# A gated group norm whose factors go to the partitions through memory instead of through products with the identity

## The chip, the core and the metric

The kernel runs on one core of a Trainium2 chip. A core has TensorE (PE, matrix products into PSUM), VectorE (DVE), ScalarE (ACT), GpSimd (POOL) and SyncE (SP, which here issues nearly all DMAs), each with its own queue of instructions, worked off in order. The metric is the device time of one execution in microseconds (us), lower is better.

## What is computed

Two layers of a decoder trunk over 512 tokens of 1024 channels, float32: a Mamba-2 mixer and a feed-forward block, then a recurrent mixer and a feed-forward block, each between RMS norms. The change lies in the first mixer, after its scan:

```python
def gated_group_rmsnorm(y, z, w):
    bsz, s, d = y.shape                                   # d = 2048
    g = (y * jax.nn.silu(z.astype(jnp.float32))).reshape(bsz, s, SSD_GROUPS, d // SSD_GROUPS)
    g = g * lax.rsqrt(jnp.mean(g * g, axis=-1, keepdims=True) + EPS)
    return g.reshape(bsz, s, d) * w.astype(jnp.float32)

def ssd_mixer(u, w_in, conv_w, conv_b, dt_bias, a_log, d_skip, norm_w, w_out):
    proj = u @ w_in
    z = proj[..., :SSD_D_INNER]
    ...
    y = ssd_chunked_scan(xs, dt, a, bm, cm)
    y = y + d_skip.astype(jnp.float32)[:, None] * xs
    y = gated_group_rmsnorm(y.reshape(bsz, s, SSD_D_INNER), z, norm_w)
    return (y.astype(u.dtype) @ w_out).astype(u.dtype)
```

So each of 4 groups of 512 channels has one factor for each of the 512 tokens.

## The kernel before

Activations lie with channels over the 128 partitions and the 512 tokens along the free dimension; y of the mixer is 16 such tiles, 4 to a group, held in pairs in the buffers named w and v. Every large product is made of three fp32r products of split operands (high times high, high times low, low times high): `up_mm` (L241 to L248) makes 24 matmuls for a tile of 128 output channels, and `Weight` (L214 to L236) loads 512 KB of weights through SP (L220) into one of 4 buffers r, and splits it with ACT (L227) and DVE (L228).

`ssd` (L333) walks over the 4 groups. For each group `scan_group` works through 4 chunks of 128 tokens. `scores` loads cs_d spread over the partitions (L435), makes products L437, turns y tiles with the identity (L443), and computes decays on ACT (L459, L460, L466) and DVE (L439, L445, L461, L467). `products` makes the short products L477 and L479 and adds their result to y on DVE (L486). Between the chunks stand "fill" units: projections with convolution for the next group (`conv_tile`: ACT L327, DVE L329, ACT L415, DVE L416), and the gate of the group before.

`gate(g)` has three steps. `project` multiplies y by silu(z) and sums the squares of the 4 tiles into one tile, sq, of 128 partitions by 512 tokens (DVE L525, L528; ACT L524, L529; POOL L533). `rate` sums sq over the partitions with a column of ones (L540, result r: tokens on partitions, 4 columns), adds eps on DVE (L541) and raises it to -1/2 on POOL (L543). Then r must get from "token on the partition" to "token along the free dimension, the same on all partitions": `rate` copies r along the free dimension into sq (L544), and `scale` multiplies that by the identity on PE (L550), so that the factors stand in a PSUM bank, which DVE reads while it scales the 4 tiles of y (L554). The four gates are called "places" below: the first runs in the fill of group 2, the second in that of group 3, the third after the last scan, and the fourth among the products with the output weights (L665), after which ACT and DVE split the scaled y (L259, L260).

The order on each engine is made by a scheduler at build time, which places instructions by its own estimate of when they can run. PSUM banks are split into 4 for projections (M) and 4 for the rest (X), each handed out in turn; the narrow buffers t come in a pool of 5 for projections and gates (C2).

Of the kernel before, what the change touches and what calls it, by code (L numbers as in the profile page):

```python
# [8 lines left out]
F32 = mybir.dt.float32  # L9
F32R = mybir.dt.float32r  # L10
AF = mybir.ActivationFunctionType
ALU = mybir.AluOpType

P = 128
D = 1024
S = 512
KD = D // P
NT = S // P
DI = 2048
NH = 32  # L20
NG = 4
# [54 lines left out]
def tile_trunk(ctx: ExitStack, tc: tile.TileContext, x, norm_mix_pre, norm_mix_post, norm_ffn_pre, norm_ffn_post,  # L76
               ssd_w_in, ssd_conv_w, ssd_conv_b, ssd_dt_bias, ssd_a_log, ssd_d, ssd_norm, ssd_w_out,
               lru_w_in, lru_b_in, lru_conv_w, lru_conv_b, lru_w_gx, lru_b_gx, lru_w_ga, lru_b_ga,
               lru_lambda, lru_w_out, lru_b_out, ffn_w_up, ffn_conv_w, ffn_conv_b, ffn_w_down, out, layers=4):
# [3 lines left out]
    V, A, G, T = nc.vector, nc.scalar, nc.gpsimd, nc.tensor  # L83
    dma = nc.sync.dma_start
# [44 lines left out]
    ident, nhalf, ones = (small_tiles[n] for n in ("ident", "nhalf", "ones"))  # L129
# [8 lines left out]
    def small():  # L138
        return stats[:, stat_ids.pop(0), :]
# [98 lines left out]
    def up_w(w, c0, n=P, lo=None, hi=None):  # L238
        return Weight([w[:, c0:c0 + n].rearrange("(k p) c -> p k c", p=P)], KD, KD * n, lo, hi)

    def up_mm(pt, w, h, tok, m=P, by_k=True):  # L241
        o = pt.ap[0:m, :].rearrange("p (a b) -> p a b", a=2)[:, tok, :]
        hh, hl = (a[:, tok, :, :] for a in h)
        ops = ((w.wh, hh), (w.wh, hl), (w.wl, hh))
        todo = [(k, i) for k in range(KD) for i in range(3)] if by_k else [(k, i) for i in range(3) for k in range(KD)]
        for n, (k, i) in enumerate(todo):
            last = T.matmul(o, ops[i][0][:, k, :], ops[i][1][:, :, k, :], start=(n == 0), stop=(n == 3 * KD - 1))  # L247
        return last  # L248
# [84 lines left out]
    def ssd(h, prep, fetch, epilogue):  # L333
        w_in, w_out = ssd_w_in[0], ssd_w_out[0]
        M, X = PS.take(4), PS.take(4)
# [3 lines left out]
        def y_of(m):  # L339
            return y[m // 2].ap[:, cols(m % 2)]  # L340
# [6 lines left out]
        pt = M.get()  # L347
# [30 lines left out]
        v, e_, z, z2, p_, one = (s.ap[0:NH, :] for s in ts_)  # L378
# [11 lines left out]
        pt = X.get()  # L390
# [7 lines left out]
        pt = X.get()  # L398
# [113 lines left out]
                cur = nxt  # L512


        def gate(g):
            st = {}

            def project(m):
                w = up_w(w_in, m * P)
                pt = M.get()  # L520
                up_mm(pt, w, h, FULL)
                w.free()
                th = C2.get()
                A.activation(th.ap, pt.ap, AF.Tanh, scale=0.5)  # L524
                V.scalar_tensor_tensor(out=th.ap, in0=th.ap, scalar=1.0, in1=pt.ap, op0=ALU.add, op1=ALU.mult)  # L525
                pt.free()
                ym = y_of(m)
                V.scalar_tensor_tensor(out=ym, in0=th.ap, scalar=0.5, in1=ym, op0=ALU.mult, op1=ALU.mult)  # L528
                A.activation(th.ap, ym, AF.Square)  # L529
                if m == 4 * g:  # L530
                    st["sq"] = th
                else:
                    G.tensor_tensor(out=st["sq"].ap, in0=st["sq"].ap, in1=th.ap, op=ALU.add)  # L533
                    th.free()

            def rate():
                sq, r = st["sq"], small()
                pt = X.get()
                for t in range(NT):
                    T.matmul(pt.ap[:, t:t + 1], sq.ap[:, t * P:(t + 1) * P], ones[:, 0:1], start=True, stop=True)  # L540
                V.tensor_scalar(out=r, in0=pt.ap[:, 0:NT], scalar1=1.0 / 512, scalar2=EPS, op0=ALU.mult, op1=ALU.add)  # L541
                pt.free()
                G.tensor_tensor(out=r, in0=r, in1=nhalf, op=ALU.pow)  # L543
                V.tensor_copy(sq.ap.rearrange("p (a b) -> p a b", a=NT), r.unsqueeze(2).to_broadcast([P, NT, P]))  # L544

            def scale():
                sq = st["sq"]
                pt = X.get()
                for t in range(NT):
                    T.matmul(pt.ap[:, t * P:(t + 1) * P], sq.ap[:, t * P:(t + 1) * P], ident, start=True, stop=True)  # L550
                sq.free()
                for m in range(4 * g, 4 * g + 4):
                    ym = y_of(m)
                    V.scalar_tensor_tensor(out=ym, in0=ym, scalar=consts["clru"][:, 100 + m:101 + m], in1=pt.ap, op0=ALU.mult, op1=ALU.mult)  # L554
                pt.free()

            return [lambda m=m: project(m) for m in range(4 * g, 4 * g + 4)], rate, scale

        def conv_units(g):
# [24 lines left out]
        with behind(marks + turned), tc.issue_after(first_fetch.ins):  # L584
            dma(dall, ssd_d.to_broadcast([P, NH]))
            for e in range(2):
                V.tensor_copy(dch[64 * e:64 * e + 64, :], dall[64 * e:64 * e + 64, :].rearrange("p (m e) -> p e m", e=2)[:, e, :])
            rows_late()
        gates = [gate(g) for g in range(NG)]
        for g in range(NG):  # L590
            nxt = conv_units(g + 1) if g < NG - 1 else None
# [3 lines left out]
            elif g < NG - 1:  # L595
                z, rate, scale = gates[g - 1]
                z, u = list(z), fill
# [10 lines left out]
        z, last_rate, last_scale = gates[NG - 1]  # L608
        z[0]()
        gates[NG - 2][1]()  # L610
        z[1]()
        gates[NG - 2][2]()
        z[2]()
        z[3]()


        ya = []
# [199 lines left out]
    consts = {}  # L817
# [115 lines left out]
    for ph in range(layers):  # L933
# [26 lines left out]
        if ph == 0:  # L960
            ssd(h, prep, fetch, epilogue)
        elif ph == 2:
            lru(h, prep, fetch, epilogue)
        else:
            ffn(ph // 2, h, prep, fetch, epilogue)
# [31 lines left out]
```

## Time and profile before

| | us |
|---|---|
| median of 3 runs | 1641.8 (1641.77 to 1642.23) |
| the profiled execution | 1640.5 |
| its span in the profile | 1638.7 |
| PE busy | 1626.4 |
| DVE busy | 925.3 |
| ACT busy | 705.0 |
| POOL busy | 175.2 |

Busy time is per engine; the engines overlap. PE's weight loads (PEld) run beside its products. The granted clock of PE is at full in all 40 slices of the page. A row of a timeline merges instructions of one line that follow each other, and its brackets say how long the engine stood idle before the row and what ended that. The first mixer takes about the first 400 us of the span.

### The profile page before, as it was taken

To read this page: it belongs to the slowest core of one execution; us is meant where nothing else is said; L and a number is where in the kernel's file an instruction comes from. 1 tells how busy PE (TensorE), PEld (TensorE's weight loads), DVE (VectorE), ACT (ScalarE), POOL (GpSimd) and SP (SyncE) were. 2 spreads that over 40 slices of the span, in tenths; PEclk is the share of its full clock that TensorE was granted. 3 is DMA by queue.
4 is the path that set the end of the run, shared out by engine and by line. 5 is a ranking of instruction groups with operands and counts; after the bars stand their busy time and mean duration, and the time that the engine had idled before them with its cause. 6 is when DMAs were issued, how large, how long until landed. Compare 5 with 4: busy or idle time off the path is not lost.

```text
span 1638.7 us, 20013 instructions
## 1 busy us (share of the span) xinstructions
PE 1626.4 (99%) x7925; PEld 1352.9 (83%) x7925; DVE 925.3 (56%) x1204; ACT 705.0 (43%) x1036; POOL 175.2 (11%) x194
## 2 busy tenths in 40 slices
PE   8999999999999999999999999999999999999998
PEld 7877887888888888888888988879888888888886
DVE  7979888546644444443343687967444444443342
ACT  5476754334533333332333478546333333333331
POOL 1023113102111111100000100011111101100001
PEclk9999999999999999999999999999999999999999
DMA  7444441333623322323334033436322323233321
GB/s 206 113 122 115 117 120 47 103 104 99 179 81 94 87 83 85 90 91 103 104 116 129 14 107 101 129 94 167 91 84 83 90 79 101 78 90 96 119 69 52
DMA packets 235419, 165.21 MB, mean 101 GB/s; under 512 B 6576, under 2 KB 219292, under 8 KB 235327
## 3 DMA queue, kind: packets, MB, share of 16 engines
q1 hardware_dynamic: 235038, 163.68, 34.5%
q8 instruction: 62, 1.02, 0.3%
q14 instruction: 31, 0.25, 0.0%
q10 hardware_dynamic: 288, 0.26, 0.0%
HBM read 161.76 MB, written 2.16 MB: 100 GB/s over the span
## 4 chain that ended last, share of the span: by engine, by line
PE 95%; DMA 2%; ACT 1%; DVE 1%; POOL 1%; issue 0%; SPq 0%; POOLq 0%; DVEq 0%; ACTq 0%
PE ps L247 60%; PE ps L270 25%; PE ps L665 5%; DMA w<-cs_d 1%; PE ps L188 1%; PE ps L477 1%; PE ps L479 1%; PE ps L491 0%; ACT w L459 0%; POOL t L533 0%; PE ps L443 0%; PE ps L699 0%; PE ps L700 0%; PE ps L701 0%; PE ps L354 0%
## 5 line engine op out<-in xcount | busy, mean ns | idle before, releaser
L247 PE MATMUL ps<-hh,w 128*128 128x512 f32 (+1 forms) x3248 | 945.8, 376 | 0.0
L247 PEld LDWEIGHTS ps<-hh,w 128*128 128x128 f32 x3248 | 592.1, 189 | 110.1 <-issue 3.0
L228 DVE TENSOR_TENSOR w<-r,w 128x1024 fp32r<-128x1024 f32 x281 | 346.6, 1239 | 539.3 <-ACT w L227 329.2
L247 PE MATMUL ps<-hl,w 128*128 128x512 f32 (+1 forms) x1624 | 603.6, 376 | 0.0
L227 ACT ACTIVATE w<-r 128x1024 fp32r<-128x1024 f32 (+1 forms) x280 | 292.9, 1054 | 368.2 <-PE ps L247 149.1
L270 PE MATMUL ps<-w,w 128*128 128x512 f32 x1776 | 405.8, 390 | 0.0
L270 PEld LDWEIGHTS ps<-w,w 128*128 128x128 f32 x1776 | 332.8, 188 | 70.2 <-issue 1.4
L247 PEld LDWEIGHTS ps<-hl,w 128*128 128x128 f32 x1624 | 303.0, 188 | 54.9 <-issue 2.0
L804 POOL TENSOR_TENSOR w<-t,t 128x512 f32<-128x512 f32 x48 | 61.6, 1283 | 461.8 <-DVE t L329 452.2
L329 DVE SCALAR_TENSOR_TENSOR t<-ps,cffn1a,t 128x511 f32<-128x511 f32 (+1 forms) x128 | 95.5, 746 | 17.6 <-ACT t L327 15.5
L329 DVE SCALAR_TENSOR_TENSOR t<-ps,cffn0a,t 128x511 f32<-128x511 f32 (+1 forms) x128 | 95.5, 746 | 15.9 <-ACT t L327 13.8
L327 ACT ACTIVATE t<-ps,cffn1b 128x512 f32<-128x512 f32 x64 | 49.4, 771 | 92.5 <-PE ps L247 92.5
L665 PE MATMUL ps<-w,w 128*128 128x512 f32 x384 | 88.5, 391 | 0.0
L327 ACT ACTIVATE t<-ps,cffn0b 128x512 f32<-128x512 f32 x64 | 49.4, 771 | 90.2 <-PE ps L247 90.2
L665 PEld LDWEIGHTS ps<-w,w 128*128 128x128 f32 x384 | 71.7, 188 | 15.0 <-DVE w L228 0.2
L799 ACT ACTIVATE t<-t 128x512 f32<-128x512 f32 x64 | 40.4, 632 | 92.8 <-DVE t L329 92.8
L259 ACT ACTIVATE w<-w 128x512 fp32r<-128x512 f32 (+1 forms) x62 | 40.2, 650 | 69.2 <-PE ps L270 40.0
L202 POOL TENSOR_SCALAR stats<-stats 128x1 f32<-128x1 f32 x32 | 9.1, 286 | 552.5 <-ACT t L200 552.5
L459 ACT ACTIVATE w<-w,t 128x128 f32<-128x128 f32 x128 | 39.3, 391 | 36.6 <-DMA w<-cs_d 33.6
L329 DVE SCALAR_TENSOR_TENSOR t<-ps,cssd,t 128x511 f32<-128x511 f32 (+2 forms) x72 | 52.4, 737 | 2.5 <-ACT t L327 2.3
L260 DVE TENSOR_TENSOR w<-w,w 128x512 fp32r<-128x512 f32 (+1 forms) x62 | 44.5, 718 | 8.2 <-ACT w L259 8.2
L200 ACT ACTIVATE t<-ps 128x512 f32<-128x512 f32 x32 | 19.1, 598 | 57.9 <-PE ps L270 50.7
(185 smaller groups left out, 904.1 us busy)
## 6 DMA issues: line engine op xcount, KB each, us to landing
r<-in_ffn_w_up_dram SPq DMA_DIRECT2D x128, 512.0 KB, 4.1
r<-in_ffn_w_down_dram SPq DMA_DIRECT2D x64, 512.0 KB, 3.4
r<-in_ssd_w_in_dram SPq DMA_DIRECT2D x40, 512.0 KB, 3.8
r<-in_lru_w_in_dram SPq DMA_DIRECT2D x20, 512.0 KB, 4.9
w<-cs_d SPq DMA_DIRECT2D x16, 512.0 KB, 8.7
r<-in_ssd_w_out_dram SPq DMA_DIRECT2D x16, 512.0 KB, 3.8
r<-in_lru_w_out_dram SPq DMA_DIRECT2D x10, 512.0 KB
out_dram<-xr SPq DMA_DIRECT2D x6, 256.0 KB, 2.0
```

Of the source, the lines that this page charges most:

```text
L227: A.activation(self.hi.ap[:, 0:n], r, AF.Copy)
L228: (lo or V).tensor_tensor(out=self.lo.ap[:, 0:n], in0=r, in1=self.hi.f[:, 0:n], op=ALU.subtract)
L247: last = T.matmul(o, ops[i][0][:, k, :], ops[i][1][:, :, k, :], start=(n == 0), stop=(n == 3 * KD - 1))
L259: A.activation(self.ah, ap, AF.Copy)
L260: V.tensor_tensor(out=self.al, in0=ap, in1=self.ah.bitcast(F32), op=ALU.subtract)
L270: T.matmul(acc[h].ap, x_[:, tk], w_[:, cols(h)], start=(first and i == 0), stop=(last and i == 2))
L327: A.activation(dst, src, AF.Identity, bias=col(k) if bias is None else bias, scale=col(k - 1))
L329: V.scalar_tensor_tensor(out=dst[:, s:S], in0=src[:, 0:S - s], scalar=col(k - 1 - s), in1=dst[:, s:S], op0=ALU.mult, op1=ALU.add)
L459: A.activation(scv[:, e, :], csv[:, e, :], AF.Relu, scale=-1.0, bias=csT[:, c, 8 * g + e:8 * g + e + 1])
L665: T.matmul(acc.ap, a[:, tk], b[:, u, :], start=(j == 0 and u == 0 and i == 0), stop=(j == 7 and u == 1 and i == 2))
L799: A.activation(ga.ap, ga.ap, AF.Gelu_apprx_tanh)
L804: G.tensor_tensor(out=p[-1].ap[:, cols(m % 2)], in0=ga.ap, in1=va.ap, op=ALU.mult)
```

## The change

`rate` no longer copies r into sq. It writes r, 128 partitions by 4 columns, as a row of 512 tokens into a buffer in memory (r_d, one row for each group), and reads that row back into sq, spread over all 128 partitions. Both transfers are issued by SP, and the second waits for the first to have landed. `scale` multiplies y by sq directly, without PE and without a PSUM bank; sq stays in use until the scaling is done. At the end of the scan the scaling of group 2 is written after the last three projections of group 3.

```diff
+        r_d = tc.dram_tile([NG, S], F32, name="r_d")
+
...
                 G.tensor_tensor(out=r, in0=r, in1=nhalf, op=ALU.pow)
-                V.tensor_copy(sq.ap.rearrange("p (a b) -> p a b", a=NT), r.unsqueeze(2).to_broadcast([P, NT, P]))
+
+                dma(r_d[g].rearrange("(t p) -> p t", p=P), r)
+                dma(sq.ap, r_d[g:g + 1].to_broadcast([P, S]))
 
             def scale():
                 sq = st["sq"]
-                pt = X.get()
-                for t in range(NT):
-                    T.matmul(pt.ap[:, t * P:(t + 1) * P], sq.ap[:, t * P:(t + 1) * P], ident, start=True, stop=True)
-                sq.free()
                 for m in range(4 * g, 4 * g + 4):
                     ym = y_of(m)
-                    V.scalar_tensor_tensor(out=ym, in0=ym, scalar=consts["clru"][:, 100 + m:101 + m], in1=pt.ap, op0=ALU.mult, op1=ALU.mult)
-                pt.free()
+                    V.scalar_tensor_tensor(out=ym, in0=ym, scalar=consts["clru"][:, 100 + m:101 + m], in1=sq.ap, op0=ALU.mult, op1=ALU.mult)
+                sq.free()
...
         z, last_rate, last_scale = gates[NG - 1]
         z[0]()
         gates[NG - 2][1]()
-        z[1]()
+        for m in range(1, 4):
+            z[m]()
         gates[NG - 2][2]()
-        z[2]()
-        z[3]()
```

The scheduler makes a new order from this. Three pieces of it follow; each row is a line, an operation, and output and input tiles with their numbers. In the order of the change the lines are those of the changed file (L547 and L548 there are the two transfers; the other lines named here are the same as before).

DVE at the first place, before:

```order
L541 TENSOR_SCALAR stats<-ps_241_1626 128x4
L416 SCALAR_TENSOR_TENSOR v_39_438<-t_247_1666,t_246_1665 128x512
L544 COPY t_170_1197<-stats 128x512
L228 TENSOR_TENSOR w_298_1971<-r_296_1968,w_297_1970 128x1024
L439 TENSOR_TENSOR t_43_445<-ps_258_1745,mask 128x128
L461 TENSOR_TENSOR w_263_1760<-w_263_1760,t_43_445 128x1024
L329 SCALAR_TENSOR_TENSOR t_252_1704<-ps_251_1679,cssd,t_252_1704 128x511
L554 SCALAR_TENSOR_TENSOR w_34_433<-w_34_433,clru,ps_254_1712 128x512 x2
L554 SCALAR_TENSOR_TENSOR w_35_434<-w_35_434,clru,ps_254_1712 128x512 x2
```

and with the change:

```order
L416 SCALAR_TENSOR_TENSOR v_39_438<-t_247_1668,t_246_1667 128x512
L228 TENSOR_TENSOR w_297_1968<-r_295_1965,w_296_1967 128x1024
L554 SCALAR_TENSOR_TENSOR w_34_433<-w_34_433,clru,t_170_1198 128x512
L329 SCALAR_TENSOR_TENSOR t_252_1706<-ps_251_1681,cssd,t_252_1706 128x511
L554 SCALAR_TENSOR_TENSOR w_34_433<-w_34_433,clru,t_170_1198 128x512
L554 SCALAR_TENSOR_TENSOR w_35_434<-w_35_434,clru,t_170_1198 128x512 x2
L486 SCALAR_TENSOR_TENSOR w_36_435<-w_36_435,dch,ps_254_1718 128x128 x2
L486 SCALAR_TENSOR_TENSOR w_37_436<-w_37_436,dch,ps_254_1718 128x128 x2
L439 TENSOR_TENSOR t_43_445<-ps_257_1742,mask 128x128
L329 SCALAR_TENSOR_TENSOR t_252_1706<-ps_251_1681,cssd,t_252_1706 128x510
L467 TENSOR_TENSOR w_281_1871<-w_281_1871,w_158_1138 128x1024
L461 TENSOR_TENSOR w_262_1757<-w_262_1757,t_43_445 128x1024
```

The copy L544 is gone, the first scaling L554 stands where it was the turn of L439 and L461, and these two come after all four scalings and L486.

SP at the first place, before:

```order
L220 DMA r_333_2192<-in_ssd_w_in_dram 128x8x128
L435 DMA w_275_1846<-cs_d 128x8x128
L220 DMA r_340_2239<-in_ssd_w_in_dram 128x8x128
L435 DMA w_302_2007<-cs_d 128x8x128
L435 DMA w_324_2140<-cs_d 128x8x128
```

and with the change:

```order
L220 DMA r_332_2189<-in_ssd_w_in_dram 128x8x128
L435 DMA w_274_1843<-cs_d 128x8x128
L547 DMA r_d<-stats 128x4x1
L548 DMA t_170_1198<-r_d 128x512
L220 DMA r_339_2237<-in_ssd_w_in_dram 128x8x128
L435 DMA w_301_2004<-cs_d 128x8x128
```

The write and the read back stand between a load of cs_d and the next weight load.

PE at the first place, before:

```order
L437 MATMUL ps_258_1745<-w_158_1137 128x128
L247 MATMUL ps_267_1777<-hh_83,w_265_1773 128x512
L247 MATMUL ps_267_1777<-hl_84,w_265_1773 128x512
L247 MATMUL ps_267_1777<-hh_83,w_266_1774 128x512
L247 MATMUL ps_267_1777<-hh_83,w_265_1773 128x512
L247 MATMUL ps_267_1777<-hl_84,w_265_1773 128x512
L477 MATMUL ps_255_1721<-w_230_1547,t_229_1545 64x128
```

and with the change, at the same stretch:

```order
L247 MATMUL ps_251_1681<-hh_83,w_249_1677 128x512
L247 MATMUL ps_251_1681<-hl_84,w_249_1677 128x512
L247 MATMUL ps_251_1681<-hh_83,w_250_1678 128x512
L477 MATMUL ps_254_1718<-w_230_1548,t_229_1546 64x128
L479 MATMUL ps_254_1718<-w_231_1559,t_234_1585 64x128
```

A later stretch of PE with the change, where the y tile v_39 is turned:

```order
L247 MATMUL ps_288_1897<-hh_83,w_286_1893 128x512
L247 MATMUL ps_288_1897<-hl_84,w_286_1893 128x512
L443 MATMUL ps_258_1745<-ident,v_39_438 128x128
L443 MATMUL ps_276_1848<-ident,v_39_438 128x128
L247 MATMUL ps_288_1897<-hh_83,w_287_1894 128x512
```

Before, L437 and five products L247 stood ahead of the short products L477 and L479, and L550 among these; now the short products come first, and L443, which needs the finished tile v_39, comes 71 products L247 after them.

## Rows read from the trace of the kernel before

**Rows 1.** The page: busy time of each engine (share, instructions), and the chain by engine.

```profile
PE 1626.4 (99%) x7925; PEld 1352.9 (83%) x7925; DVE 925.3 (56%) x1204; ACT 705.0 (43%) x1036; POOL 175.2 (11%) x194
...
PE 95%; DMA 2%; ACT 1%; DVE 1%; POOL 1%; issue 0%; SPq 0%; POOLq 0%; DVEq 0%; ACTq 0%
```

**Rows 2.** The chain in order of time: start us, us, engine, tile and line.

```profile
171.76 0.44 DVE t L544
172.24 1.16 PE ps L550 x8
...
194.81 1.03 PE ps L477 x16
...
240.30 0.89 PE ps L550 x8
...
291.41 0.89 PE ps L550 x8
292.30 10.89 PE ps L247 x48
...
336.79 0.89 PE ps L550 x8
```

**Rows 3.** Timeline of PE's weight loads: start us, us; in brackets idle before, and releaser.

```profile
172.24 0.41 PEld L550 LDWEIGHTS ps<-ident,t 128*128 128x128 f32 x3 [0.36 <-DVE t L544]
```

**Rows 4.** Timeline of DVE around the first place, same columns.

```profile
173.23 0.28 DVE L439 TENSOR_TENSOR t<-ps,mask 128x128 f32<-128x128 f32 x1
173.55 1.23 DVE L461 TENSOR_TENSOR w<-w,t 128x1024 f32<-128x1024 f32 x1
176.46 0.75 DVE L329 SCALAR_TENSOR_TENSOR t<-ps,cssd,t 128x511 f32<-128x511 f32 x1 [1.68 <-ACT t L327]
177.13 2.72 DVE L554 SCALAR_TENSOR_TENSOR w<-w,clru,ps 128x512 f32<-128x512 f32 x4
...
180.42 1.12 DVE L486 SCALAR_TENSOR_TENSOR w<-w,dch,ps 128x128 f32<-128x128 f32 x4
181.45 1.22 DVE L467 TENSOR_TENSOR w<-w,w 128x1024 f32<-128x1024 f32 x1
```

**Rows 5.** Timeline of POOL, first place.

```profile
170.32 1.41 POOL L543 TENSOR_TENSOR stats<-stats,nhalf 128x4 f32<-128x4 f32 x1 [10.33 <-DVE stats L541]
```

**Rows 6.** Timeline of SP: first the write of cs_d, then the first place.

```profile
74.43 0.34 SPq L389 DMA_DIRECT2D cs_d<-t  x1
76.07 2.84 SPq L435 DMA_DIRECT2D w<-cs_d  x3
...
173.40 0.37 SPq L220 DMA_DIRECT2D r<-in_ssd_w_in_dram  x1
174.89 4.78 SPq L435 DMA_DIRECT2D w<-cs_d  x2
```

**Rows 7.** DMA view: queue; issues (count, KB each, median us to landing).

```profile
q1 hardware_dynamic: 235038, 163.68, 34.5%
...
w<-cs_d SPq DMA_DIRECT2D x16, 512.0 KB, 8.7
...
out_dram<-xr SPq DMA_DIRECT2D x6, 256.0 KB, 2.0
...
v<-in_norm_mix_post_dram SPq DMA_DIRECT2D x2, 512.0 KB, 3.7
```

**Rows 8.** Timeline of ACT, first place.

```profile
181.01 2.46 ACT L459 ACTIVATE w<-w,t 128x128 f32<-128x128 f32 x8 [1.74 <-DMA w<-cs_d]
...
186.69 0.62 ACT L415 ACTIVATE t<-t 128x512 f32<-128x512 f32 x1
```

**Rows 9.** Timeline of PE, start of the short products of the first place.

```profile
171.25 0.45 PE L477 MATMUL ps<-w,t 128*64 128x128 f32 x4
```

**Rows 10.** Timeline of DVE at the second and the fourth place.

```profile
241.91 2.71 DVE L554 SCALAR_TENSOR_TENSOR w<-w,clru,ps 128x512 f32<-128x512 f32 x4
...
326.00 1.23 DVE L228 TENSOR_TENSOR w<-r,w 128x1024 fp32r<-128x1024 f32 x1 [3.54 <-PE ps L665]
```

## The prediction

> **What bounds the kernel now.** I read the page's busy shares first: TensorE (PE) is busy 99% of 1638.7 us, and 95% of the chain that ended last is PE time, DMA 2% [rows 1]. So an instruction taken off PE shortens the kernel by its own time, and work on other engines counts only where PE comes to wait for it. Then the four places where the group norm runs, one for each group of channels. In the chain in order of time, the products with the identity (L550) stand there with their whole length, and at the first of them the chain passes through the copy that feeds them (L544) [rows 2]. The weight loads of PE show 0.36 us of waiting for that copy [rows 3]. The third view is VectorE's (DVE) own timeline around the first place, since DVE is where the new wait will stand.
>
> **The change, part by part.** *PE.* Sixteen fp32 products go (32 records, 8 to a place): 1.16 + 0.89 + 0.89 + 0.89 = 3.83 us [rows 2], and the wait of 0.36 us before the first goes with them [rows 3]. Two of the four places lie among the short products L477 and L479, where the joins come out slightly differently; I round 4.19 down to 4.0 us. PE's other instructions stay, in another order, and I put that at nothing: the changes from one kind of product to another are nearly as many as before.
>
> *DVE.* Four copies of 0.44 us go [rows 2]. DVE is not the bound, so this is worth nothing by itself. The scaling L554 keeps its instructions, 2.72 us for four [rows 4], and reads SBUF where it read PSUM; I put that at nothing.
>
> *The chain that takes the place of copy and products.* GpSimd (POOL) ends the power at 170.32 + 1.41 = 171.73 at the first place [rows 5]. From there it was 0.44 us of copy and 1.16 us of products. Now SyncE (SP) writes r to memory, waits until it has landed, and issues the read back. The nearest row for the first transfer is the write of cs_d: issued at 74.43, and the first read of it could be issued at 76.07, so 1.64 us [rows 6]. That is the lower end; cs_d goes in 32 rows of 2 KB, r in 512 pieces of 4 bytes. The hardware queue's 235038 packets took 34.5% of 16 engines' 1638.7 us, 38 ns each on average [rows 7]; 512 of them over 16 engines are 32 x 38 ns = 1.2 us, so the upper end is 2.9 us. I take 2.2. The read back is 128 rows of 2 KB, 256 KB. Its nearest rows are out_dram, 256 KB in 2.0 us, and the spread gain norm_mix_post, 512 KB in 3.7 us [rows 7]; I take 2.8. The far row is the spread of cs_d, 512 KB in 8.7 us [rows 7]. With 0.1 us for signals the chain is 5.1 us, between 3.7 and 6.7, and 11.7 at the far end.
>
> The Trainium skill ("DMA: Bandwidth & Descriptors", Rules for kernel authors) says that a strided last dimension lowers to one descriptor per element and should be rearranged, which speaks against this write; the order shows the 128x4x1 pattern, and no row here has a transfer of 4-byte pieces. Its fit (Anatomy of one DMA) of 2.0 us plus bytes at 436 GB/s would give, as an estimate, 2.0 + 2.6 = 4.6 us for the chain, and the same sum below; the write of cs_d at 1.64 us is under its constant.
>
> *SP's queue.* SP issues in order, so whatever stands behind the write waits for POOL, and what stands behind the read waits for the landing. At the first place that is the weight load which went out at 173.40, now about 174.4, and the load of cs_d at 174.89, which keeps its time [rows 6]. At the second and third place the next weight load waits longer for a free buffer anyway; at the fourth one load comes some 3 us later, with weights needed 20 us on. So nothing comes from the queue itself, but at the first place a spread of 256 KB now lies ahead of cs_d in the engines, and I let that data come 1 us later than 181.01, where ScalarE (ACT) waited for it [rows 8].
>
> *The first place.* This is the tight one. By the order DVE now runs L228 and then stands at the first L554 until the chain ends: 171.73 + 5.1 = 176.8. Before, it did L439 and L461 in that time, and began L554 at 177.13 [rows 4]. L439 and L461 now come after the four L554 and L486. From 176.8 to the end of the L416 that completes convolution tile v_39, the order has four L554 (2.72), three L329 (0.75 each), four L486 (1.12), L439 (0.28), three L467 (1.22 each), L461 (1.23), L228 (as long as L467, it has the same size), one L525 and one L416 (as one L554, 0.7 each): 13.9 us by [rows 4]. Starts follow each other some 0.08 us before the end (181.45 follows 180.42 by 1.03, where four L486 take 1.12 [rows 4]), which takes off 1.0: L416 ends at 189.7. On the ACT side, from the landing of cs_d to the end of L415, which feeds L416, it took 186.69 + 0.62 - 181.01 = 6.3 us [rows 8]; the new order has one L466 more in between, about 1 us, so 182.0 + 7.3 + 0.7 for L416 = 190.0, nearly the same. PE must turn that tile 71 products L247 after it began the short products of this chunk. Those began at 171.25 [rows 9]; five L247 and one L437 now stand behind them, so they begin at about 169.9. Then 16 short products, twice the 1.03 us that eight took (16 records) at 194.81, 71 L247 at 10.89 / 48 = 0.227 us = 16.1, and nine products or turns of the size of L550, 0.89 / 4 = 0.22 us each = 2.0 [rows 2]: 190.1. So here cover is nil: what the chain or cs_d comes later than I take is lost on PE. With the chain at 3.7 nothing is lost, at 6.7 some 1.6 us, and cs_d by itself may cost up to 2. I take 0.9 us.
>
> *The other three places.* At the second the scaling moves ahead of two convolution tiles; it ran at 241.91 [rows 10], and now runs when its chain ends, about 236, in a stretch where DVE waits anyway. The next turned tile leaves about 2 us of cover. At the third the order puts three projections, 72 L247 or 16.3 us, between the sums and the first product with the output weights; cover 4 to 5 us. At the fourth DVE stood idle for 3.54 us before 326.00 [rows 10]; the scaling fits there, and PE needs the result after 72 products more; cover about 4 us.
>
> *Sum.* 0.9 - 4.0 = -3.1 us. The profiled execution took 1640.5 us, its span 1638.7; 1640.5 - 3.1 = 1637.4. The median of the runs is 1641.8, 1.3 us above it, so 1638.7. Two tenths of a per cent, about what a measurement of this kernel can tell from no change, are 3.3 us, so the boundary to faster is 1638.5.
>
> **The rivals.** *All is hidden.* The chain takes 4.5 us or less, or PE comes to that turn later than I reckon, and the whole 4.0 us is left: 1637.8. For it speaks that after the first place PE has no waits of note; against it that the cover there is nil by my sum.
>
> *Slower: the read back is as slow as the spread of cs_d.* Both read one short piece of memory for 128 partitions, beside weight loads. With 1.64 + 8.7 + 0.1 = 10.4 us the chain is 5.3 us longer than I take. At the first place the loss is then 0.9 + 5.3 = 6.2 us, at the second 5.3 - 2 = 3.3, at the third and fourth about 1 each: 11.5 us, against 4.0 gained, so +7.5: 1649.3. It turns slower by 0.2% when the losses pass 7.3 us, from a chain of about 9.3 us on. Against it: cs_d is twice the bytes in 512-byte pieces, and the gain, which is spread in long pieces, takes 3.7 us [rows 7].
>
> *The strided write is what is slow.* One element to a piece at twice the mean packet's time, 76 ns, would be 32 x 76 ns = 2.4 us on top of 1.64; the chain is then 7.0 us, the first place loses 0.9 + 1.9 = 2.8, and 1.2 us of gain are left: 1640.6. The Trainium skill's rule on strided dimensions ("DMA: Bandwidth & Descriptors", Rules for kernel authors) points to this case, and no run here shows it yet.
>
> *More than expected.* The new order also removes small waits of PE elsewhere in the mixer (half a microsecond here and there): 1637.0.
>
> That the change doesn't do what it says is excluded by the order: no L550 is left, and the eight new transfers stand on SP.
>
> **How the numbers follow.** Forecast, part of the gain given back at the first place: 0.45; all hidden: 0.29; slow write: 0.08; slow read back: 0.12; more: 0.06. The forecast's own range is 1637.8 to 1639.8, most of it above 1638.5: I count 0.10 of its 0.45 as faster. Faster: 0.10 + 0.29 + 0.06 = 0.45. Slower: 0.12. Same: 0.43. The range that leaves out the slow read back and the better half of the last case runs from 1637.0 to 1641.8.
>
> **What would show it.** The eight transfers on SP, and from the end of POOL's power to the first L554 about 5 us; the issue of the read back 1.7 to 3 us after that of the write. DVE waits at the first L554 for a DMA for about 5 us at the first place, at the fourth for as much without harm. PE shows a wait of about 1 us at the L443 of v_39 near 190, and none at the other places. ACT gets cs_d about 1 us later than 181.01. The span shrinks by about 3 us, all of it between 165 and 345 us, and the rest of the trace keeps its lengths. I am wrong if PE waits somewhere behind a weight load, if DVE stands longer than 7 us at an L554, or if the gain is lost again at the hand-over to the first feed-forward layer.

## The result, and the profile after

The changed kernel takes 1663.7 us (median; 1663.2 to 1664.5) against 1641.8 before: a ratio of 1.0137, with a 95% interval of 1.0125 to 1.0149. It is 22 us slower. I had forecast 1638.7 and a range that ended at 1641.8.

The page of the changed kernel, by engine and along the chain that ended last; compare [rows 1]:

```profile
span 1661.4 us, 19954 instructions
PE 1630.4 (98%) x7893; PEld 1352.7 (81%) x7893; DVE 921.7 (55%) x1200; ACT 704.2 (42%) x1036; POOL 178.0 (11%) x194
PE 87%; DMA 5%; DVE 3%; ACT 2%; issue 1%; POOL 1%; SPq 0%; POOLq 0%; DVEq 0%; ACTq 0%
```

PE's share of the chain fell from 95% to 87%; the shares of DMA, DVE and ACT rose from 2, 1 and 1% to 5, 3 and 2%. Where that happens the table by stages tells (first row: the kernel before; columns: stretch, its length, busy time of PE, PEld, DVE, ACT and POOL with instruction counts, granted clock, DMA share, GB/s):

```profile
160.00:370.00 210.00, 209.88 (x1168) 171.50 (x1167) 146.02 (x208) 101.98 (x175) 34.32 (x27) 1.00 0.35 100
...
160.00:395.00 235.00, 216.98 (x1147) 174.53 (x1146) 144.13 (x206) 103.37 (x177) 36.97 (x27) 0.96 0.37 101
180.00:200.00 20.00, 12.83 (x48) 10.00 (x47) 13.70 (x21) 9.02 (x17) 0.00 (x0) 0.83 0.42 118
260.00:280.00 20.00, 18.70 (x86) 14.87 (x87) 17.63 (x28) 12.13 (x22) 5.15 (x4) 0.83 0.38 106
320.00:340.00 20.00, 17.21 (x69) 13.76 (x69) 10.88 (x12) 7.53 (x11) 5.39 (x3) 0.91 0.51 157
```

The loss lies between 160 and 395, the stretch of the four places; ahead of it the two kernels are 0.1 us apart, and of the 22.7 us at the end 22.4 stand at its end. PE is idle there for 235.0 - 217.0 = 18 us, where the kernel before had 0.1, and in three slices the granted clock is below 1.0. At 0.83 over 20 us PE was at its lower level, 1.2 GHz, for 6.8 us; over the three slices that makes 17 us.

SP's queue at the four places (start, duration of the issue, transfer); the rows before it are [rows 6]:

```profile
171.69 0.37 SPq L547 DMA_DIRECT2D r_d<-stats  x1
181.87 0.33 SPq L548 DMA_DIRECT2D t<-r_d  x1
...
182.77 3.19 SPq L435 DMA_DIRECT2D w<-cs_d  x2
239.52 0.37 SPq L547 DMA_DIRECT2D r_d<-stats  x1
247.79 0.34 SPq L548 DMA_DIRECT2D t<-r_d  x1
302.81 0.37 SPq L547 DMA_DIRECT2D r_d<-stats  x1
313.02 0.34 SPq L548 DMA_DIRECT2D t<-r_d  x1
342.47 0.37 SPq L547 DMA_DIRECT2D r_d<-stats  x1
350.96 0.34 SPq L548 DMA_DIRECT2D t<-r_d  x1
```

From the issue of the write to that of the read back are 10.2, 8.3, 10.2 and 8.5 us, where I took 2.2. At the first place the next load of cs_d goes out at 182.77, 7.9 us later than before. What is at work in those ten microseconds? The DMA engines in 40 equal slices of 302 to 314, their busy share in tenths, and the packets:

```profile
DMA  0000016000000000000000000000000000000000
DMA packets 528, 0.00 MB, mean 0 GB/s; under 512 B 528, under 2 KB 528, under 8 KB 528
```

The 512 pieces (and 16 more packets) are through in two slices of 0.3 us, about 1.3 us after the issue at 302.81. After that nothing moves until the read back is issued at 313.02. So the time isn't in moving the pieces; it is between the last piece and the signal that the write is done.

What the engines make of it at the first place (DVE, PE and ACT; in brackets the idle time before a row and what ended it):

```profile
185.81 0.75 DVE L554 SCALAR_TENSOR_TENSOR w<-w,clru,t 128x512 f32<-128x512 f32 x1 [13.89 <-DMA t<-r_d]
...
189.12 1.12 DVE L486 SCALAR_TENSOR_TENSOR w<-w,dch,ps 128x128 f32<-128x128 f32 x4
...
183.21 0.39 PE L247 MATMUL ps<-hh,w 128*128 128x512 f32 x1
190.39 0.77 PE L437 MATMUL ps<-w 128*128 128x128 f32 x2 [6.79 <-DVE w L486]
...
192.45 1.05 PE L247 MATMUL ps<-hh,w 128*128 128x512 f32 x2
193.30 0.63 PE L247 MATMUL ps<-hl,w 128*128 128x512 f32 x1
...
196.65 0.63 PE L247 MATMUL ps<-hh,w 128*128 128x512 f32 x2
197.12 0.39 PE L247 MATMUL ps<-hl,w 128*128 128x512 f32 x1
...
190.62 2.46 ACT L459 ACTIVATE w<-w,t 128x128 f32<-128x128 f32 x8 [10.91 <-DMA w<-cs_d]
```

DVE stands at L554 for 13.9 us. Behind it in DVE's order is L486, and PE's next L437 waits for it; PE stops for 6.8 us. L437 doesn't read what L486 writes. It needs the PSUM bank that L486 reads: by the kernel's text the four banks X go to the short products (read by L486), to one L437, to the turned tiles L443, to L450, and then again to this L437. In the kernel before, L486 began at 180.42 and took 1.12 us [rows 4], and the same L437 stood 3.5 us behind its end:

```profile
185.08 0.38 PE L437 MATMUL ps<-w 128*128 128x128 f32 x2
```

When PE starts again in the changed kernel it is at the lower clock: two products take 0.85 us from start to start (192.45 to 193.30), and 0.47 four microseconds later (196.65 to 197.12). PE's waits from 160 to 370 (us in total, times, longest) show the other places:

```profile
PE ps L437 <- DVE w L486: 6.8, 1, 6.8
PE ps L443 <- DVE v L416: 4.8, 2, 4.4
PE ps L664 <- DVE t L527: 4.3, 2, 2.7
...
```

6.8 and 0.4 us fall on the first place, 4.4 on the second and 4.3 on the third; the three rows left out, 2.2 us in all, are the fourth, at L664. With 18.1 us these are the idle time. In the stretches at half clock PE worked for 14.5 us (5.2, 5.9 and 3.4); with products every 0.43 us instead of every 0.23, that is some 6.8 us lost, an estimate. Together 24.9, less the 4.2 us of products and wait that are gone: 20.7 of the 22.7 us by which the span grew. The other 2 us are not assigned.

### The profile page after: what moved, and what is told of

It is laid out like the page before. It is cut to its first block, busy times and chain, and to the rows that moved or that the text cites. A ratio compares the mean times of both kernels' runs of the same rounds, so it can differ in the third digit from the quotient of the medians.

```text
span 1661.4 us, 19954 instructions
## 1 busy us (share of the span) xinstructions
PE 1630.4 (98%) x7893; PEld 1352.7 (81%) x7893; DVE 921.7 (55%) x1200; ACT 704.2 (42%) x1036; POOL 178.0 (11%) x194
## 4 chain that ended last, share of the span: by engine, by line
PE 87%; DMA 5%; DVE 3%; ACT 2%; issue 1%; POOL 1%; SPq 0%; POOLq 0%; DVEq 0%; ACTq 0%
PE ps L247 55%; PE ps L270 24%; PE ps L664 4%; DMA r_d<-stats 2%; DMA w<-cs_d 2%; PE ps L188 1%; DMA t<-r_d 1%; DVE w L228 1%; ACT w L459 1%; POOL t L535 0%; PE ps L477 0%; POOL stats L545 0%; DVE w L260 0%; PE ps L491 0%; DVE v L554 0%
## 5 line engine op out<-in xcount | busy, mean ns | idle before, releaser
L247 PE MATMUL ps<-hh,w 128*128 128x512 f32 (+1 forms) x3248 | 948.2, 376 | 0.0
L247 PEld LDWEIGHTS ps<-hh,w 128*128 128x128 f32 x3248 | 593.7, 189 | 110.7 <-issue 2.3
L247 PE MATMUL ps<-hl,w 128*128 128x512 f32 (+1 forms) x1624 | 604.4, 376 | 0.0
L247 PEld LDWEIGHTS ps<-hl,w 128*128 128x128 f32 x1624 | 303.9, 189 | 55.2 <-issue 2.3
L329 DVE SCALAR_TENSOR_TENSOR t<-ps,cffn1a,t 128x511 f32<-128x511 f32 (+1 forms) x128 | 95.4, 746 | 18.0 <-ACT t L327 15.9
L329 DVE SCALAR_TENSOR_TENSOR t<-ps,cffn0a,t 128x511 f32<-128x511 f32 (+1 forms) x128 | 95.3, 746 | 15.9 <-ACT t L327 13.8
L664 PE MATMUL ps<-w,w 128*128 128x512 f32 x384 | 91.2, 397 | 6.5 <-DVE t L527 4.3
L664 PEld LDWEIGHTS ps<-w,w 128*128 128x128 f32 x384 | 72.8, 191 | 23.5 <-DVE t L527 5.2
L329 DVE SCALAR_TENSOR_TENSOR t<-ps,cssd,t 128x511 f32<-128x511 f32 (+2 forms) x72 | 52.4, 737 | 1.2 <-ACT t L327 1.0
```

Source lines behind the costliest of these rows:

```text
L329: V.scalar_tensor_tensor(out=dst[:, s:S], in0=src[:, 0:S - s], scalar=col(k - 1 - s), in1=dst[:, s:S], op0=ALU.mult, op1=ALU.add)
L664: T.matmul(acc.ap, a[:, tk], b[:, u, :], start=(j == 0 and u == 0 and i == 0), stop=(j == 7 and u == 1 and i == 2))
```

## Experiments

**The form of the write.** Two versions change nothing but how r goes to memory. In the first, r is stored in the order it has in SBUF, 128 pieces of 16 bytes, and the scaling reads the spread row with a stride:

```
-                dma(r_d[g].rearrange("(t p) -> p t", p=P), r)
+                dma(r_d[g].rearrange("(p t) -> p t", t=NT), r)
...
-     in1=sq.ap
+     in1=sq.ap.rearrange("p (q t) -> p t q", t=NT)
```

> The changed kernel with one thing altered: r is stored in the order it has in SBUF (128 pieces of 16 bytes instead of 512 pieces of 4 bytes), and the scaling reads the spread row with a stride of four elements. Theory A (what the write costs is its number of pieces): the step from the issue of the write to that of the read back falls from 8.2-10.2 us to 2.5-4 us, the wait of DVE at the first L554 of each place from 9.4-14.0 us to 3-7 us, PE's waits at the four places from about 19 us to under 3, no stretch at half clock is left, and the time comes to 1638-1646 us. Theory B (any write to memory that is read straight back takes 8 us or more, whatever its pieces): the step stays at 8-10 us and the time at 1660-1665 us. Theory C (the read back is what is slow): the step falls little, the time stays over 1655 us.

In the second, PE turns r into four rows of 512 bytes first:

```
-                dma(r_d[g].rearrange("(t p) -> p t", p=P), r)
+                T.transpose(pt.ap[0:NT, 0:P], r, ident)
+                V.tensor_copy(sq.ap[0:NT, 0:P], pt.ap[0:NT, 0:P])
+                dma(r_d[g].rearrange("(t p) -> t p", p=P), sq.ap[0:NT, 0:P])
```

> The changed kernel, with r turned on PE (one 128x4 transpose a place) and copied to four rows of 512 bytes before the write, so that the write has 4 pieces and not 512. Theory A (pieces): the write takes 1.6-2.2 us to the issue of the read back, as cs_d's write did, the turn and copy put about 1 us ahead of it, PE pays 4 x 0.1-0.3 us, and the time comes to 1638-1646 us. Theory B (any write that is read straight back is slow): write still 8-10 us, time 1660-1666 us.

1643.6 us (ratio to before 1.0015, 1.0006 to 1.0024) and 1641.4 us (1.0002, 0.9993 to 1.0012). Some 20 of the 22 us are gone with the 4-byte pieces, in both. SP at the first two places of the first version, and at the first place of the second:

```profile
171.33 0.34 SPq L547 DMA_DIRECT2D r_d<-stats  x1
174.75 0.33 SPq L548 DMA_DIRECT2D t<-r_d  x1
233.61 0.34 SPq L547 DMA_DIRECT2D r_d<-stats  x1
235.90 0.34 SPq L548 DMA_DIRECT2D t<-r_d  x1
```

```profile
178.01 0.27 SPq L551 DMA_DIRECT2D r_d<-t  x1
179.19 0.34 SPq L552 DMA_DIRECT2D t<-r_d  x1
```

The write takes 3.4 and 2.3 us in the first version, 1.2 in the second (3.8 at its second place). Theory A holds against B and C on the write and the time. Neither version gains, though. In the first one scaling (L554, there L555) takes 1.14 us with the stride instead of 0.75, and PE still waits 5.3 us in all, where theory A had under 3. In the second PE still stops at the first place, for 2.2 us, since its write is issued only at 178.01: the copy that feeds it stands in DVE's order behind an L329 that waits for ACT until 177.01. Half clock for 6.8 us follows there in the profiled execution, which was the slowest of ten (1643.7 us); in most of the others the mean granted clock was 0.999 or more, so they can't have had such a stretch.

**The order alone.** The last edit of the diff in the kernel before, three projections ahead of the third scaling:

```
         gates[NG - 2][1]()
-        z[1]()
+        for m in range(1, 4):
+            z[m]()
         gates[NG - 2][2]()
-        z[2]()
-        z[3]()
```

> The kernel before with the last edit of the diff alone: the three projections of the last group ahead of the third scaling; the products with the identity stay. My theory: 1640.5-1643 us, no difference to before, since PE stays fed. Rival: the order itself costs some of the 22 us, by a wait of PE at the first products with the output weights (4.65 us there in the changed kernel): 1645-1648 us.

1641.1 us, ratio 1.0001 (0.9991 to 1.0011). The order costs nothing by itself.

**What is slow in a 4-byte write.** A chain of transfers behind the last output of the kernel before, each issued when the one ahead has landed:

```
+    dma(pd[k, 0:512].rearrange("(t p) -> p t", p=P), px.ap[:, 0:4])
+    dma(px.ap[:, 0:512], pd[k:k + 1, 0:512].to_broadcast([P, S]))
...
+    dma(pd[k].rearrange("(t p e) -> p t e", p=P, e=P)[:, :, 0:1], px.ap[:, 0:4].rearrange("p (t e) -> p t e", e=1))
+    dma(px.ap[0:1, 0:1], pd[k:k + 1, 0:1])
```

> The kernel before with a chain of transfers on SP's queue after its last output, each waiting for the one ahead, with nothing else on the DMA engines; from issue to issue gives what each takes. Theory A1 (each small piece costs time at the end of the write, wherever it goes): 512 pieces of 4 bytes 8-10 us when they lie in one 2 KB row and the same when they lie 512 bytes apart, 256 pieces 4-5 us, 128 pieces 2.5-3.5 us, 512 pieces of 64 bytes 8-10 us, 4 pieces of 512 bytes about 2 us. Theory A2 (many small writes into the same few lines of memory are what is slow): dense 8-10 us, the pieces 512 bytes apart 2-3 us, the 64-byte pieces 2-3 us. Theory B (every write read back is slow): all 8 us or more. The read back of one row by 128 partitions: 3.6-4.3 us as in the changed kernel if it is the spread that sets it, about 2.0 us if it was the weights beside it.

Four of its writes on SP, each with the read that waits for it: 512 pieces of 4 bytes side by side (L977), 128 of 16 bytes (L980), 512 of 4 bytes that lie 512 bytes apart (L986), 128 of 4 bytes side by side (L992):

```profile
1660.43 0.37 SPq L977 DMA_DIRECT2D probe_d<-v  x1
1668.40 0.32 SPq L973 DMA_DIRECT2D v<-probe_d  x1
1673.70 0.32 SPq L980 DMA_DIRECT2D probe_d<-v  x1
1675.10 0.32 SPq L973 DMA_DIRECT2D v<-probe_d  x1
...
1682.92 0.37 SPq L986 DMA_DIRECT2D probe_d<-v  x1
1684.78 0.24 SPq L975 DMA_DIRECT2D v<-probe_d  x1
...
1696.09 0.33 SPq L992 DMA_DIRECT2D probe_d<-v  x1
1703.56 0.23 SPq L975 DMA_DIRECT2D v<-probe_d  x1
```

From write to read: 8.0, 1.4, 1.9 and 7.5 us. Three more: 4 pieces of 512 bytes 1.2, 256 of 4 bytes side by side 7.5, 512 of 64 bytes far apart 1.8. Theory A2 holds against A1 and B. The number of pieces isn't it, nor their size alone, since 512 pieces of 4 bytes far apart take 1.9. It is small pieces that lie side by side. That 128 cost as much as 256 was in neither theory, and two more chains followed it up; they differ from this one in the forms and in that each write is followed by the read of one element.

> The kernel before with a second chain of writes behind its last output, each followed by a read of one element that waits for it; only the form of the write differs. The first chain gave 8 us for 512 pieces of 4 bytes side by side, 7.5 us for 128 of them, and 1.9 us for 512 that lie 512 bytes apart, so the count isn't it. Theory A2 (what is slow is that pieces from different partitions fall into the same short stretch of memory): at 8 and 16 bytes apart still 6-8 us, at 64 and 128 bytes apart 1.9 us; 8-byte pieces side by side 6-8 us, 64-byte pieces 1.9 us. Theory A3 (the pieces must touch): already 8 bytes apart 1.9 us. For 4-byte pieces side by side the time falls to about 1.2 us somewhere between 128 and 1 pieces: if each stretch of memory is settled by itself and at the same time as the others, 16 pieces still cost 7 us; if they queue for one place, the cost falls with their number.

> The kernel before with a third chain of writes of 4-byte pieces behind its last output, to see what it is that the pieces queue for. The second chain gave, for pieces side by side, 7.2 us with 64 from 64 partitions, 3.6 with 32, 1.3 with 16. Theory M (they queue for a stretch of memory of about 256 bytes, some 0.1 us each): 64 pieces side by side cost about 7 us also when they come from 16, 8 or 4 partitions; the same 64 pieces in four groups of 16 that lie 512 bytes apart cost 1.3-2 us, in two groups of 32 about 3.6; four groups of 64 about 7; 48 side by side about 5.5, 24 about 2.5. Theory N (what counts is how many partitions, so how many of the 16 engines, write at the same time): 64 pieces from 16 partitions cost 1.3-2 us whether side by side or in groups, from 32 partitions about 3.6 either way, and the grouping changes nothing.

The results of both, from issue to issue (4-byte pieces, unless said; the stretch of 256 bytes is the one that the grouping points to):

| form of the write | pieces in 256 bytes | us |
|---|---|---|
| 512 side by side | 64 | 9.1 |
| 512, 8 bytes apart | 32 | 2.9 |
| 512, 16 bytes apart | 16 | 2.7 |
| 512, 64 bytes apart | 4 | 1.8 |
| 512 of 8 bytes side by side | 32 | 4.0 |
| 512 of 16 bytes side by side | 16 | 2.5 |
| 512 of 64 bytes side by side | 4 | 1.8 |
| 64 side by side, from 64 partitions (three times) | 64 | 7.2, 7.3, 6.8 |
| 64 side by side, from 32, 16, 8 and 4 partitions | 64 | 6.0, 6.5, 8.2, 7.6 |
| 48, 32, 24 and 16 side by side | 48, 32, 24, 16 | 6.1, 3.3, 2.4, 1.3 |
| 4 groups of 64, 32 and 16, groups 512 bytes apart | 64, 32, 16 | 8.0, 3.4, 1.4 |

In the second chain both theories missed in the middle: pieces 8 bytes apart took 2.9 us, where A2 had 6 to 8 and A3 1.9, and the time fell with the number of pieces side by side (64, 32, 16). In the third, theory M holds and N falls: 64 pieces from 16 partitions cost 6.5 us side by side and 1.4 in four groups. The four rows of the third chain that decide it, 64 pieces from 16 partitions side by side and then in groups:

```profile
1655.44 0.32 SPq L973 DMA_DIRECT2D probe_d<-v  x1
1661.91 0.21 SPq L974 DMA_DIRECT2D v<-probe_d  x1
1664.37 0.32 SPq L973 DMA_DIRECT2D probe_d<-v  x1
1665.77 0.21 SPq L974 DMA_DIRECT2D v<-probe_d  x1
```

So the times are as if pieces that fall into the same 256 bytes or so settled one after another, about 0.1 to 0.15 us each ((6.0 - 1.3) / 48 and (6.1 - 1.3) / 32, from 16 pieces up), and different stretches at the same time. The rule is rough: 64 pieces took from 6.0 to 8.2 us, and at 16 in a stretch 512 pieces took 2.5 to 2.7 us where 16 took 1.3. What does the settling, and whether it also happens with pieces from one partition, no run shows. r has 64 pieces in each of its eight stretches, which fits the 8.2 to 10.9 us that its write took from SP in all the runs.

**One place at a time.** The products back at the first place, then memory at the first place alone (the same with `g == 0`); `scale` has the products under the same condition:

```
+                if g > 0:
                     dma(r_d[g].rearrange("(t p) -> p t", p=P), r)
                     dma(sq.ap, r_d[g:g + 1].to_broadcast([P, S]))
+                else:
+                    V.tensor_copy(sq.ap.rearrange("p (a b) -> p a b", a=NT), r.unsqueeze(2).to_broadcast([P, NT, P]))
```

> The changed kernel with the first of the four places as it was (copy and products with the identity), the other three through memory with the 4-byte write. My theory: each place has its own price, read in the changed kernel as the shift of landmarks behind it (8.4 us for the first, about 2.5, 5.5 and 6 us for the others): 1640.8 + 14 = 1655 us (1652-1658), with no half clock before 240. Rival: the places are not independent, what the first loses covers the later ones (the weights are further ahead after a stall), so that without it the others lose more: 1659-1663 us.

> The kernel before with the first place alone through memory with the 4-byte write (and the order edit, which by itself made no difference). My theory: 1640.8 + 8.4 = 1649 us (1647.5-1651), PE waits about 7 us at the L437 behind L486 and runs at half clock for 5 us after it. Rival (places depend on each other): 1643-1646 us, as the later stages have slack to take it back.

1658.9 us (ratio 1.0107, 1.0092 to 1.0123) and 1651.8 us (1.0066, 1.0049 to 1.0083). The first place alone costs 10.3 us, the other three 17.4: more than 22 together, so my sum by places was wrong in both. The writes took from 8.2 to 10.9 us from one place and run to the next, and half clock came for other lengths (17 us in the first version at three places, as many as at all four in the changed kernel). With the first place alone PE's waits are 10.1 us, where they were 7.2 at that place in the changed kernel; with the other three, 12.4 (the products' own wait left out) where they were 10.9. Whether that explains all of the difference stays open.

**Another queue.** Both transfers issued by POOL:

```
-                dma(r_d[g].rearrange("(t p) -> p t", p=P), r)
-                dma(sq.ap, r_d[g:g + 1].to_broadcast([P, S]))
+                nc.gpsimd.dma_start(r_d[g].rearrange("(t p) -> p t", p=P), r)
+                nc.gpsimd.dma_start(sq.ap, r_d[g:g + 1].to_broadcast([P, S]))
```

> The changed kernel with both transfers of r issued from POOL's queue in place of SP's, so that the weights and cs_d behind them on SP are not held up. Theory S (the data in sq comes late for DVE, and that is enough): DVE still stands at L554 until about 187, PE's wait at the first place stays 6-7 us, the time 1658-1665 us. Rival Q (SP held up, so cs_d and weights late, is what costs): cs_d goes out near 175 again and the time falls to 1645-1652 us. If the write takes another time from this queue, the sum goes by the step from its issue to the read back.

1670.5 us, ratio 1.0176 (1.0156 to 1.0197). SP is free, and cs_d goes out early, though its data lands only at 187.37; POOL's write is slower still:

```profile
173.51 6.96 SPq L435 DMA_DIRECT2D w<-cs_d  x2
173.02 0.99 POOL L547 DMA_DIRECT2D r_d<-stats  x1 [0.30 <-POOL stats L545]
185.89 0.58 POOL L548 DMA_DIRECT2D t<-r_d  x1 [11.87 <-DMA r_d<-stats]
192.25 2.74 DVE L554 SCALAR_TENSOR_TENSOR w<-w,clru,t 128x512 f32<-128x512 f32 x4 [12.35 <-DMA t<-r_d]
187.37 2.45 ACT L459 ACTIVATE w<-w,t 128x128 f32<-128x128 f32 x8 [7.13 <-DMA w<-cs_d]
```

DVE stands 12.4 us at L554 and PE 12.5 us behind it, until 201.44, and cs_d was there 4.9 us before sq. That the data in sq is late is enough, as theory S says, and rival Q falls; but wait and time lie above what S gave, with a step of 12.9 us here, more than on SP. In this version's order L486 stands ahead of L554, and PE waits at an L443 for the L416 that completes its tile, the kind of wait that I had foreseen.

**Versions that use it.** The first place with copy and products, as in the diff above; the others with the turn, the copy and the write of four rows, as in the second version of the write:

> A version made from what the runs showed: the first place keeps the copy and the products with the identity; at the other three r is turned on PE, written as four rows of 512 bytes and read back spread. My theory: the chain there is about 1 us of turn and copy, 1.5-3.7 us of write and 3-4 us of read back, which the projections behind the sums cover, so PE gains 3 x 0.89 us less three turns of 0.1-0.2 us: 2.2 us under before (1637.8-1640 us beside a before of 1641). Rival: PE's wait only moves to the second or fourth place, or the other order of instructions costs what is gained: 1640.5-1643 us.

1638.0 us beside 1641.3: ratio 0.9980 (0.9971 to 0.9989). It beats both kernels. It and the version with the first place back (1.0107) differ in the form of the write and its turn alone, and lie 21 us apart. Its second place, on SP and DVE:

```profile
236.92 0.47 SPq L552 DMA_DIRECT2D r_d<-t  x1
240.55 0.35 SPq L553 DMA_DIRECT2D t<-r_d  x1
243.69 2.74 DVE L567 SCALAR_TENSOR_TENSOR w<-w,clru,t 128x512 f32<-128x512 f32 x4 [1.68 <-DMA t<-r_d]
```

The write still takes 3.6 us among other traffic, the data is there 3.1 us later, and PE's only wait left in the stretch is 0.3 us, at the products of the first place.

A version without memory spreads r by fp32r products of a matrix of ones with a diagonal of r:

```
+                V.tensor_tensor(out=sq.ap.rearrange("p (a b) -> p a b", a=NT), in0=ident.unsqueeze(1).to_broadcast([P, NT, P]), in1=r.unsqueeze(2).to_broadcast([P, NT, P]), op=ALU.mult)
+                st["d"] = Act(sq.ap, LO)
...
+                T.matmul(pt.ap, small_tiles["onesr"][:, 0:1].to_broadcast([P, P]), d.ah, start=True, stop=False)
+                T.matmul(pt.ap, small_tiles["onesr"][:, 0:1].to_broadcast([P, P]), d.al, start=False, stop=True)
```

> A version without memory: in place of the copy and four fp32 products a place, a diagonal of r (one product on DVE), split into two fp32r parts (a copy on ACT, a difference on DVE), and two fp32r products of a matrix of ones with it. PE takes 2 x 0.227 us a place instead of 0.89-1.16, so 2.0 us less in all; DVE takes 1.4 us a place instead of 0.44, ACT 0.6 more, and the chain from POOL's power to the products is some 1.5 us longer. Theory: hidden at three places, at the first place up to 1 us lost: 1639-1641 us beside a before of 1641. Rival: the longer chain on DVE costs more at the first place than PE gains: 1641.5-1644 us.

1651.2 us, ratio 1.0055 (1.0043 to 1.0068): worse than either theory. PE waits 2.9 us at an L443 until 175.5, followed by half clock for 6.8 us. That is less than the 10 us lost; the diagonal takes slots of the split weights, which changes the order elsewhere too, but what the rest is stays open.

## Why the prediction was wrong

*What bounds the kernel.* Right, and shown by the other side of the change too: with the products gone at three places and nothing to wait for, PE's busy time falls from 1626.4 to 1622.3 us and the kernel's time with it. For the version with rows at three places I reckoned 2.2 us, and it gave 3.4 (1.8 to 4.8 by the interval).

*The write: the step that failed.* I bounded it by 1.64 us from the write of cs_d and 2.9 us from the mean time of a packet [rows 6, 7], and took 2.2. It took 8.3 to 10.2. The first is a whole write, completion included, but of another form; the second adds the time in which pieces move, and the pieces did move in that time, within 1.3 us of the issue at the third place and 2.1 to 2.6 at the others. The row of cs_d could not show the rest: no two of its 32 pieces of 2 KB share a stretch of 256 bytes. My rival of the slow write named the right transfer but priced it again by packets, 76 ns each, and so came to 1640.6. The case that a completion could cost more than the transfer was in none of my bounds.

The Trainium skill ("DMA: Bandwidth & Descriptors", Rules for kernel authors) advises against a strided last dimension, which lowers to one descriptor per element. The direction was right, but the number of descriptors isn't what costs here: 512 elements 512 bytes apart are done in 1.9 us. Nearer is what the Trainium skill says on the same page (Anatomy of one DMA), for DMAs issued from GpSimd: most of a transfer's fixed cost is the wait for the target memory to confirm the write. The trace agrees in kind, with the engines idle after the last piece, but for nearly 9 us at the third place, where the Trainium skill has about 2 in all; and the write issued from POOL, for which its fit is made, took 9.6 to 12.9 us.

*The read back.* I took 2.8, from 2.0 to 3.7. It took 3.7 to 4.4 us to the start of L554, at my upper row or beyond it. In the quiet chain the same spread took 3.0 to 3.8 us after a write of 16 or 512-byte pieces, and 4.7 and 5.3 after the dense one, so part of that is the write's too. The chain was 12.4 to 14.1 us in all, beyond even my far end of 11.7, where my rule for the slow rival (slower from 9.3 us on) already said slower. DVE stood 9.4 to 14.0 us at L554, and more than 7 was my own sign of being wrong.

*SP's queue, "nothing".* Wrong with a chain of that length: cs_d went out at 182.77 instead of 174.89, and ACT had it at 190.6 instead of 181.01 [rows 6, 8]. This was not what decided: PE's stop ended at 190.39 with L486, before ACT began with cs_d, and in the run on POOL's queue PE stood longer though cs_d landed before sq.

*The first place.* The cover was nil, as I had it, but I looked for the wait at the L443 of tile v_39. It came before that, at L437, because L486, which frees the PSUM bank that L437 needs, stands behind L554 in DVE's order. I had listed L486 in that very queue and not asked who waits for it.

*The other places.* The covers of 2 to 5 us were of the right order: with chains of 12.4 to 13.9 us PE waited 4.4, 4.3 and 2.2 us, and with chains of 6.1 to 6.8 us, in the version with rows at three places, nothing.

*PE's clock.* It has no term in my sum. During or right after stalls of 2.7 to 6.8 us the granted clock fell to 1.2 GHz for 3.4 to 6.8 us, by the estimate above 6.8 us of the loss.

## What to carry to other kernels

A small transfer is priced by what its pieces do where they land, not by its bytes or its packets: where no row of a trace has such pieces, the upper bound is open, and a chain that something waits for should not rest on it. Turn a column of values into a few long rows before it goes to memory, and send it through memory only where the work behind it covers some 7 us. When an instruction is made to wait in an engine's order, ask for each instruction behind it who waits for it, for its result or for the buffer or bank that it frees; and give a long stall of PE a second price, the products at half clock after it.

## What the runs showed of the hardware

- Writes of 64 and more 4-byte pieces side by side complete 5 to 9 us after their last piece has gone; the time from issue goes with the pieces in the same 256 bytes or so (16: 1.3 us, 32: 3.3 to 3.6, 48: 6.1, 64: 6.0 to 8.2) and little with their number in all (128 to 512: 7.5 to 9.1). It doesn't go with the partitions they come from, and on POOL's queue it was no shorter (9.6 to 12.9 us in the kernel, from SP's 8.2 to 10.9).
- A spread of one 2 KB row to 128 partitions takes 3.0 to 3.8 us on idle DMA engines (4.7 and 5.3 behind a dense write of 4-byte pieces), while 256 KB of separate rows were read in 2.6 us.
- A 128x512 scaling on DVE took 0.75 us with its row read in order and 1.14 us with a stride of 16 bytes.
